# Second attention: the reciprocals of a pair of heads, spread over partitions by TensorE or by transfers through DRAM

## The chip, the cores and the metric

One core of one Trainium2 chip. The metric is the device time of one execution in microseconds; the time of before is the median of three runs, 1263.89 us (1263.47 to 1264.3).

## The reference, cut to what matters

Two layers of a decoder with 512 positions and 1024 features, in float32. The second layer's mixer is an attention of 16 heads over 128 latent columns, each query keeping its best keys by an indexer. What the change touches is the end of its softmax:

```
logits = einsum(q, k) * scale + bias         # per head: 512 queries x up to 512 keys
p = softmax(logits, axis=-1)                 # exp(l - max) / sum over keys
o_lat = einsum(p, lat)
o = einsum(o_lat, w_uv)                      # 64 columns per head
```

The kernel computes exp(l - max) without dividing, takes the weighted sum of the values, and multiplies the result by the reciprocal of the sum.

## The kernel before, in words

Scores are kept with 128 queries on partitions and the keys along a row; a head has four query blocks j = 0 to 3, of 128, 256, 384 and 512 keys (causal). The sums, and so their reciprocals, stand as a [128 x 4] tile: query within the block on partitions, block along the row. The output is wanted the other way round: two heads at a time ("a pair"), 64 output columns of each on 128 partitions and the 512 queries along the row. So each pair's 2 x 512 reciprocals must become a [128 x 512] tile `bs` in which the rows 0 to 63 all hold the first head's 512 reciprocals and 64 to 127 the second's.

The loop `for h in range(HEADS)` (L1537) does the end of head h together with the scores and the softmax of head n = h + 1, in one order that is written out by hand; each engine works its queue in that order. Per head:

- `logits` (L1427) writes scores z on TensorE (PE) for a block, in one of two PSUM banks of tag "z"; `softmax` (L1430) turns them on VectorE (DVE) into L and the row minima nm (L1436, L1438); `expo` (L1441) takes the exponential on ScalarE (ACT, L1444) and its sum. Blocks 0 and 1 come first, blocks 2 and 3 after the filler `fill(mid)`; the exponential of block 3 comes last.
- `transposed` (L1448) turns head h's exponentials on PE in three groups (L1455) and copies them out (L1460 on ACT, L1462 on DVE).
- In odd heads `pair_values` (L1466) multiplies the latent rows by two heads' columns into `pv` (L1470), copied out as `vals` by ACT (L1474). In even heads `weighted` (L1476) forms the pair's output `av` for the two heads before.
- `sums` (L1532) takes the reciprocals; after an odd head `pair_sums` (L1490) copies each reciprocal 64 times into `rvb` (L1492, DVE). In the next even head `pair_scale` (L1497) transposes rvb four times into `bc` (L1501, PE) and copies it out as `bs` (L1503, ACT). `pair_hi` (L1505) multiplies av by bs (L1507) and rounds (L1510), `pair_lo` (L1513) keeps the rest (L1514).
- `fill` (L1387) puts steps of a projection between (`pt_q`, later `pt_o`; three matmuls a step), `serve` and `serve_late` (L1401, L1410) the vector work that goes with them, with `q_sum` (L1124), the split of the next weight chunk (`whi`, L208) and the fetch of the one after it (L177). `load_bias` (L1183) loads a head's bias tile `th` from DRAM. All transfers here are issued by SyncE (SP), in order.

PSUM has eight banks: three of tag "mm", two "z", two "tr", and a single one "x" (L132), which ssq (of `q_sum`), pv and bc take in turn. A tile can be allocated there only when the one before it has been read out.

Of the kernel before, what the change touches and what calls it, by code (L numbers as in the profile page):

```python
# [9 lines left out]
F32 = mybir.dt.float32  # L10
# [3 lines left out]
AF = mybir.ActivationFunctionType  # L14
# [6 lines left out]
S = 512  # L21
P = 128
KT = D // P
QT = S // P
# [4 lines left out]
HEADS = 16  # L29
# [90 lines left out]
def kernel_body(ctx, tc, xT, wst, cst, smalls, crow, ccol, relb, onehot, outT):  # L120
    nc = tc.nc
    act, dve, pe, pool = nc.scalar, nc.vector, nc.tensor, nc.gpsimd
# [11 lines left out]
    def ptile(shape, name, tag):  # L134
        return banks.tile(shape, F32, name=name, tag=tag, bufs=nbanks[tag])
# [3 lines left out]
    ident = cons[:, C_ID:C_ID + P]  # L139
# [11 lines left out]
    x = [xpool.tile([P, S], F32, name=f"x{f}") for f in range(KT)]  # L151
    halves = [slice(0, H2), slice(H2, S)]

    dp = ctx.enter_context(tc.tile_pool(name="dram", bufs=1, space=DRAM))
    rb = dp.tile([HEADS, 640], F32, name="rb")

    rel = cpool.tile([BUCKETS, HEADS], F32, name="rel")
    bias = {}
# [927 lines left out]
    def dsa_layer(l, first, man):  # L1086
        with ExitStack() as st:
# [36 lines left out]
            def q_sum(h):  # L1124
                q2 = Q.pop((h, 2))
                ssq = ptile([P, QT], "ssq", "x")
                for j in range(QT):
                    pe.matmul(ssq[:, j:j + 1], lhsT=q2[:, j * P:(j + 1) * P], rhs=ones1, start=True, stop=True)
                c = slice(h * QT, (h + 1) * QT)
                act.activation(msq[:, c], ssq, AF.Identity, scale=1.0 / P, bias=eps_c)  # L1130
# [52 lines left out]
            def load_bias(h):  # L1183
                th = ths[h] = raws.tile([P, D], F32, name="th", tag="raw")[:, :S]
                ov = rb[h:h + 1, 0:1]
                nc.sync.dma_start(th, bass.AP(tensor=ov.tensor, offset=ov.offset, ap=[[1, P], [1, S]]))
# [164 lines left out]
            with ExitStack() as sa:  # L1351
                ap = sa.enter_context(tc.tile_pool(name="att_d", bufs=2))
# [4 lines left out]
                heads = {}  # L1357
# [29 lines left out]
                def fill(n):  # L1387
                    for _ in range(n):
                        next(filler, None)

                def take():

                    if lows:
                        lows.pop(0)()
                    else:
                        split_lo()
                    for done in finished:
                        done()
                    finished.clear()

                def serve():  # L1401

                    for h in ripe:
                        q_sum(h)
                        scales.append(h)
                    ripe[:] = squares
                    squares.clear()
                    take()

                def serve_late():  # L1410

                    for h in scales:
                        q_norm(h, h + 1)
                    scales.clear()
                    take()
                    if chunks["n"]:
                        split_hi()
                        chunks["n"] -= 1

                def begin(h):  # L1420
                    L = ap.tile([P, LW], F32, name="L")
                    if h % 2 == 0:
                        rv = ap.tile([P, QT, 2], F32, name="rv", bufs=4)
                        heads["rv"] = rv
                    heads[h] = (L, ap.tile([P, QT], F32, name="nm"), ap.tile([P, QT], F32, name="sum"), heads["rv"], {})

                def logits(h, j):  # L1427
                    heads[h][4][j] = score_block(h, j)
# [12 lines left out]
                def expo(h, j):  # L1441
                    L, nm, sum_ = heads[h][:3]
                    ls = slice(LOFF[j], LOFF[j] + (j + 1) * P)
                    act.activation(L[:, ls], L[:, ls], AF.Exp, bias=nm[:, j:j + 1], scale=-1.0, accum_out=sum_[:, j:j + 1])  # L1444
# [3 lines left out]
                def transposed(h, pi, by_act):  # L1448
                    L = heads[h][0]
                    tr = ptile([P, S], "tr", "tr")  # L1450
                    w = TRW[pi]
                    for i, c0 in TRP[pi]:
                        for j in range(i, QT):
                            c = c0 + (j - i) * P
                            pe.transpose(tr[:, c:c + P], L[:, LOFF[j] + i * P:LOFF[j] + (i + 1) * P], ident)  # L1455
                    if pi == 0:
                        trs[h] = ap.tile([P, LW], F32, name="pT", bufs=2)
                    t = trs[h][:, TRO[pi]:TRO[pi] + w]
                    if by_act:
                        act.activation(t, tr[:, :w], AF.Copy)  # L1460
                    else:
                        dve.tensor_copy(t, tr[:, :w])  # L1462
# [26 lines left out]

                def pair_sums(rv):  # L1490
                    rvb = ap.tile([P, QT, 2, 64], F32, name="rvb", tag="bs")
                    dve.tensor_copy(rvb, rv[:, :, :, None].to_broadcast([P, QT, 2, 64]))  # L1492
                    return rvb

                pair = {}

                def pair_scale(rvb):  # L1497

                    bc = ptile([P, S], "bc", "x")
                    for j in range(QT):  # L1500
                        pe.transpose(bc[:, j * P:(j + 1) * P], rvb[:, j].rearrange("p a b -> p (a b)"), ident)  # L1501
                    bs = pair["bs"] = ap.tile([P, S], F32, name="bs")
                    act.activation(bs, bc, AF.Copy)  # L1503

                def pair_hi():  # L1505
                    bs = pair["bs"]
                    dve.tensor_mul(bs, pair["av"], bs)  # L1507
                    oh = pp.tile([P, S], F32R, name="ohi", tag="qh", bufs=QRING)
                    ol = pp.tile([P, S], F32R, name="olo", tag="ql", bufs=QRING)
                    act.activation(oh, bs, AF.Copy)  # L1510
                    O.append((oh, ol))

                def pair_lo():  # L1513
                    dve.tensor_sub(O[-1][1], pair["bs"], O[-1][0].bitcast(F32))  # L1514

                load_bias(2)
                begin(0)
                heads[0][4].update(early)
                for j in range(2):
# [7 lines left out]
                    expo(0, j)  # L1527
                fill(4)
                serve_late()
                rvb = None  # L1530

                def sums(h):  # L1532

                    dve.reciprocal(heads[h][3][:, :, h % 2], heads[h][2])
                    return pair_sums(heads[h][3]) if h % 2 else None

                for h in range(HEADS):  # L1537
                    n = h + 1
                    more = n < HEADS
                    values = h % 2 == 0 and h > 0  # L1540
                    mid, after = LATE_STEPS[h]
                    if more:
                        begin(n)
                        for j in range(2):
                            logits(n, j)
                        softmax(n, 0)
                        expo(n, 0)
                    if values:
                        weighted(h - 2)
                    transposed(h, 0, True)  # L1550
                    if more:
                        softmax(n, 1)
                        expo(n, 1)
                    if h % 2 and h > 1:
                        pair_lo()
                    serve()
                    if not more:
                        rvb = sums(h)
                        pair_values(h - 1)
                    fill(mid)  # L1560
                    if more:
                        for j in range(2, QT):
                            logits(n, j)
                            softmax(n, j)
                            if j < QT - 1:
                                expo(n, j)
                    transposed(h, 1, False)
                    if values:
                        pair_scale(rvb)
                    if more:  # L1570
                        rvb = sums(h)
                        if h % 2:
                            pair_values(h - 1)
                        expo(n, QT - 1)
                    transposed(h, 2, True)
                    if not more:
                        pair_scale(rvb)
                    elif n + 2 < HEADS:
                        load_bias(n + 2)
                    fill(after)  # L1580
                    serve_late()
                    if values:
                        pair_hi()
                weighted(HEADS - 2)
                pair_hi()
# [124 lines left out]
```

## Time and profile before

| | us |
|---|---|
| median of three runs | 1263.89 |
| the profiled execution | 1263.59 |
| its span, first to last instruction | 1261.8 |
| PE busy | 1253.6 |
| DVE busy | 926.2 |
| ACT busy | 584.4 |
| second attention's loop over heads, about | 759 to 874 of the span |

Every row of a trace gives a start and a duration in microseconds from the span's start. A matmul's duration reaches past the start of the next one, since matmuls are pipelined; distances between starts tell what one costs. An arrow in brackets names what ended an engine's idle time.

### The profile page before, as it was taken

The numbers are of one execution on the slowest core, as the hardware profiler recorded it, in microseconds if no ns is written. First come the engines' busy times: TensorE is split into PE (matmuls) and PEld (weight loads), VectorE is DVE, ScalarE is ACT, GpSimd is POOL, SyncE is SP. The second block draws the span as 40 slices with busy tenths as digits, with TensorE's granted clock in tenths as the row PEclk, the third lists the DMA queues.
The fourth block names the chain that finished last, engine by engine and source line by source line (L and its number), as shares of the span: only waits on it lengthen the run. The fifth ranks groups of instructions, "written<-read, shape, count | busy, mean of one in ns | idle before, by whom it ended". The sixth has DMA issues, their size and how long they took to land.

```text
span 1261.8 us, 17355 instructions
## 1 busy us (share of the span) xinstructions
PE 1253.6 (99%) x6566; PEld 1037.4 (82%) x6566; DVE 926.2 (73%) x1575; ACT 584.4 (46%) x1029; POOL 57.2 (5%) x171
## 2 busy tenths in 40 slices
PE   8999999999999999999999999999999999999999
PEld 5888787798888888888887788887988888888887
DVE  5889998878777877886768878887875456456653
ACT  6477666554323433433445446656544234334330
POOL 0000000000000000000002350110000000000000
PEclk9999999999999999999999999999999999999999
DMA  9644444514575575654412222133232422433221
GB/s 375 219 136 132 136 134 125 173 37 125 198 254 181 181 245 188 200 182 153 134 34 68 84 76 69 59 95 103 72 92 75 133 86 70 129 87 97 76 92 67
DMA packets 49316, 163.13 MB, mean 129 GB/s; under 512 B 5664, under 2 KB 6176, under 8 KB 49232
## 3 DMA queue, kind: packets, MB, share of 16 engines
q1 hardware_dynamic: 48800, 161.23, 40.0%
q8 instruction: 52, 0.85, 0.3%
q10 hardware_dynamic: 432, 0.79, 0.2%
q14 instruction: 32, 0.26, 0.1%
HBM read 159.86 MB, written 2.14 MB: 128 GB/s over the span
## 4 chain that ended last, share of the span: by engine, by line
PE 95%; DVE 3%; DMA 1%; issue 0%; ACT 0%; ACTq 0%; SPq 0%; DVEq 0%
PE pt_u L248 12%; PE pt_u L250 12%; PE pt_u L249 11%; PE pt_d L250 5%; PE pt_d L248 5%; PE pt_d L249 5%; PE pt_l L248 2%; PE pt_q L248 2%; PE pt_l L250 2%; PE pt_l L249 2%; PE pt_first L248 2%; PE pt_q L250 2%; PE pt_first L250 2%; PE pt_q L249 2%; PE pt_first L249 2%; PE pt_qk L248 1%
## 5 line engine op out<-in xcount | busy, mean ns | idle before, releaser
L208 ACT ACTIVATE whi<-raw 128x1024 fp32r<-128x1024 f32 (+1 forms) x206 | 205.0, 1003 | 118.7 <-PE pt_d L250 89.2
L248 PE MATMUL pt_u<-hhi,whi 128*128 128x512 f32 x640 | 249.2, 389 | 0.0
L249 PE MATMUL pt_u<-hhi,wlo 128*128 128x512 f32 x640 | 249.0, 389 | 0.0
L250 PE MATMUL pt_u<-hlo,whi 128*128 128x512 f32 x640 | 249.0, 389 | 0.0
L216 DVE TENSOR_TENSOR wlo<-raw,whi 128x1024 fp32r<-128x1024 f32 (+1 forms) x194 | 223.3, 1153 | 9.4 <-ACT whi L208 8.4
L1021 ACT ACTIVATE y<-pt_u,sm 128x512 f32<-128x512 f32 x80 | 62.2, 777 | 188.2 <-PE pt_u L250 188.2
L248 PEld LDWEIGHTS pt_u<-hhi,whi 128*128 128x128 f32 x640 | 120.1, 188 | 25.8 <-issue 1.1
L250 PEld LDWEIGHTS pt_u<-hlo,whi 128*128 128x128 f32 x640 | 120.1, 188 | 25.0
L249 PEld LDWEIGHTS pt_u<-hhi,wlo 128*128 128x128 f32 x640 | 120.1, 188 | 24.9
L1022 DVE SCALAR_TENSOR_TENSOR y<-pt_u,sm,y 128x511 f32<-128x511 f32 x80 | 59.9, 748 | 97.1 <-ACT y L1021 96.9
L248 PE MATMUL pt_d<-acthi,whi 128*128 128x512 f32 x288 | 112.0, 389 | 0.0
L249 PE MATMUL pt_d<-acthi,wlo 128*128 128x512 f32 x288 | 112.0, 389 | 0.0
L250 PE MATMUL pt_d<-actlo,whi 128*128 128x512 f32 x288 | 112.0, 389 | 0.0
L257 DVE SCALAR_TENSOR_TENSOR raw<-raw,cond 128x1024 f32<-128x1024 f32 x88 | 106.5, 1216 | 4.2 <-DMA raw<-wst 4.2
L375 DVE SCALAR_TENSOR_TENSOR x<-pt_d,mod,x 128x512 f32<-128x512 f32 x48 | 36.0, 749 | 72.8 <-PE pt_d L250 72.8
L232 ACT ACTIVATE acthi<-y 128x512 fp32r<-128x512 f32 x44 | 27.8, 632 | 105.4 <-DVE y L1040 105.4
L248 PE MATMUL pt_first<-hhi,whi 128*128 128x256 f32 (+1 forms) x200 | 64.0, 320 | 0.0
L249 PE MATMUL pt_first<-hhi,wlo 128*128 128x256 f32 (+1 forms) x200 | 62.8, 314 | 0.8 <-DVE wlo L216 0.8
L249 PEld LDWEIGHTS pt_d<-acthi,wlo 128*128 128x128 f32 x288 | 54.1, 188 | 11.3
L250 PEld LDWEIGHTS pt_d<-actlo,whi 128*128 128x128 f32 x288 | 54.1, 188 | 11.2
L248 PEld LDWEIGHTS pt_d<-acthi,whi 128*128 128x128 f32 x288 | 54.1, 188 | 11.2
L250 PE MATMUL pt_first<-hlo,whi 128*128 128x256 f32 (+1 forms) x200 | 63.0, 315 | 0.0
(258 smaller groups left out, 2505.3 us busy)
## 6 DMA issues: line engine op xcount, KB each, us to landing
raw<-wst SPq DMA_DIRECT2D x250, 512.0 KB, 3.7
raw<-wst SPq DMA_DIRECT2D x48, 384.0 KB, 3.0
th<-rb SPq DMA_DIRECT2D x16, 256.0 KB, 3.1
ada<-wst SPq DMA_DIRECT2D x4, 512.0 KB, 6.6
outT<-x SPq DMA_DIRECT2D x7, 256.0 KB, 2.0
x<-xT SPq DMA_DIRECT2D x5, 256.0 KB, 4.9
x<-xT ACTq DMA_DIRECT2D x3, 256.0 KB, 4.0
cond<-crow SPq DMA_DIRECT2D x1, 512.0 KB, 10.4
```

What stands on the lines that cost most here:

```text
L208: act.activation(hi[:, :n], raw[:, :n], AF.Copy)
L216: engine.tensor_sub(lo[:, :n], raw[:, :n], hi[:, :n].bitcast(F32))
L232: act.activation(hi, src, AF.Copy)
L248: pe.matmul(out, lhsT=whi, rhs=ahi, start=start, stop=False)
L249: pe.matmul(out, lhsT=wlo, rhs=ahi, start=False, stop=False)
L250: pe.matmul(out, lhsT=whi, rhs=alo, start=False, stop=stop)
L257: dve.scalar_tensor_tensor(raw, raw, 1.0, cond, op0=OP.mult, op1=OP.mult, accum_out=dst)
L375: dve.scalar_tensor_tensor(x[f][:, c], pt, mod[l][:, g * KT + f:g * KT + f + 1], x[f][:, c], op0=OP.mult, op1=OP.add)
L1021: act.activation(y, pt, AF.Identity, scale=cw[2], bias=sm[:, b + S_CB + c:b + S_CB + c + 1])
L1022: dve.scalar_tensor_tensor(y[:, 1:], pt[:, :S - 1], cw[1], y[:, 1:], op0=OP.mult, op1=OP.add)
```

## The change

For all pairs but the last, the reciprocals no longer go through rvb and bc. The tile rv is laid out with the head ahead of the block; `sums` only takes the reciprocal, and is called before `fill(mid)`. In odd heads `pair_rows` is called between the scores of block 3 and the second group of transposes: one transpose of the [128 x 8] tile rv into `tp`, a PSUM tile of tag "x"; a copy by ACT into `r8`, [8 x 128]; and a write of that to a DRAM tile `rd`. After `load_bias` of the same head `pair_spread` reads rd back twice, each head's row of 512 into 64 partitions of `bs`. `pair_hi` of the next even head takes that tile. The last pair, for which no further head comes, keeps `pair_sums` and `pair_scale`.

```
+    rd = dp.tile([HEADS, S], F32, name="rd")
...
-                        rv = ap.tile([P, QT, 2], F32, name="rv", bufs=4)
+                        rv = ap.tile([P, 2, QT], F32, name="rv", bufs=4)
...
+                def pair_rows(h, rv):
+
+                    tp = ptile([P, S], "tp", "x")
+                    pe.transpose(tp[:2 * QT, :P], rv.rearrange("p e j -> p (e j)"), ident)
+                    r8 = ap.tile([P, P], F32, name="r8", bufs=1)[:2 * QT]
+                    act.activation(r8, tp[:2 * QT, :P], AF.Copy)
+                    row = rd[h:h + 1, 0:1]
+                    nc.sync.dma_start(bass.AP(tensor=row.tensor, offset=row.offset, ap=[[P, 2 * QT], [1, P]]), r8)
+
+                def pair_spread(h):
+                    bs = pair["next"] = ap.tile([P, S], F32, name="bs")
+                    for e in range(2):
+                        row = rd[h + e:h + e + 1, 0:1]
+                        nc.sync.dma_start(bs[64 * e:64 * e + 64, :], bass.AP(tensor=row.tensor, offset=row.offset, ap=[[0, 64], [1, S]]))
...
                 def sums(h):
-                    dve.reciprocal(heads[h][3][:, :, h % 2], heads[h][2])
-                    return pair_sums(heads[h][3]) if h % 2 else None
+                    dve.reciprocal(heads[h][3][:, h % 2], heads[h][2])
...
                     serve()
+                    sums(h)
                     if not more:
-                        rvb = sums(h)
+                        rvb = pair_sums(heads[h][3])
                         pair_values(h - 1)
                     fill(mid)
                     if more:
...
+                        if h % 2:
+                            pair_rows(h - 1, heads[h][3])
                     transposed(h, 1, False)
-                    if values:
-                        pair_scale(rvb)
                     if more:
-                        rvb = sums(h)
                         if h % 2:
                             pair_values(h - 1)
                         expo(n, QT - 1)
...
                         load_bias(n + 2)
+                    if more and h % 2:
+                        pair_spread(h - 1)
                     fill(after)
                     serve_late()
                     if values:
+                        if more:
+                            pair["bs"] = pair.pop("next")
                         pair_hi()
```

## Rows read from the trace of the kernel before

**Rows 1.** The page: busy time of PE with its share of the span and its instructions, and the chain that ended last, by engine.

```profile
PE 1253.6 (99%) x6566; PEld 1037.4 (82%) x6566; DVE 926.2 (73%) x1575; ACT 584.4 (46%) x1029; POOL 57.2 (5%) x171
...
PE 95%; DVE 3%; DMA 1%; issue 0%; ACT 0%; ACTq 0%; SPq 0%; DVEq 0%
```

**Rows 2.** Windows of one pair of heads each: the window, its length, busy time (and instructions) of PE, PE's weight loads, DVE, ACT and POOL, then the granted clock, the DMA share and GB/s. The shortest and the longest of six.

```profile
766.00:780.30 14.30, 14.30 (x95) 11.61 (x93) 10.91 (x31) 9.29 (x27) 2.74 (x13) 1.00 0.13 32
...
824.80:842.40 17.60, 17.60 (x111) 14.51 (x110) 15.41 (x41) 10.14 (x30) 4.01 (x13) 1.00 0.34 99
```

**Rows 3.** What ended idle time from 755 to 890 us: engine, line, releaser, then us in total, times and the longest.

```profile
ACT L L1444 <- DVE nm L1438: 31.5, 29, 2.5
DVE L L1436 <- PE z L1178: 13.9, 9, 2.5
...
PE bc L1501 <- DVE rvb L1492: 0.2, 1, 0.2
```

**Rows 4.** The timeline in head 3: pv on PE, the first softmax instruction of block 2 of head 4 on DVE, its exponential and then `vals` on ACT.

```profile
776.88 1.06 PE L1470 MATMUL pv<-uvc,latf 128*128 128x128 f32 x8
...
777.84 0.61 DVE L1436 SCALAR_TENSOR_TENSOR L<-z,cols,th 128x384 f32<-128x384 f32 x1
...
779.09 0.62 ACT L1444 ACTIVATE L<-L,nm 128x384 f32<-128x384 f32 x1 [1.13 <-DVE nm L1438]
...
779.70 0.64 ACT L1474 ACTIVATE vals<-pv 128x256 f32<-128x256 f32 x2
```

**Rows 5.** The groups of instructions that the change removes from all pairs but the last: count, busy us and mean ns of one, idle time before them.

```profile
L1501 PE MATMUL bc<-cons,rvb 128*128 128x128 f32 x32 | 4.8, 273 | 0.2 <-DVE rvb L1492 0.2
L1503 ACT ACTIVATE bs<-bc 128x512 f32<-128x512 f32 x8 | 4.6, 581 | 0.4 <-PE bc L1501 0.4
...
L1492 DVE COPY rvb<-rv 128x512 f32<-128x512 f32 x8 | 3.4, 427 | 0.3
```

**Rows 6.** The chain of waits, the piece of the transposes bc in head 2: start, us on the chain.

```profile
771.52 0.44 PE bc L1501 x4
```

**Rows 7.** The timeline of PE: pv in heads 1, 5, 7, 9, 11 and 13.

```profile
763.62 1.06 PE L1470 MATMUL pv<-uvc,latf 128*128 128x128 f32 x8
...
791.91 1.06 PE L1470 MATMUL pv<-uvc,latf 128*128 128x128 f32 x8
...
806.80 1.16 PE L1470 MATMUL pv<-uvc,latf 128*128 128x128 f32 x8
...
820.87 1.06 PE L1470 MATMUL pv<-uvc,latf 128*128 128x128 f32 x8
...
838.46 1.06 PE L1470 MATMUL pv<-uvc,latf 128*128 128x128 f32 x8
...
855.21 1.06 PE L1470 MATMUL pv<-uvc,latf 128*128 128x128 f32 x8
```

**Rows 8.** The timeline of ACT: `vals` in heads 1, 5, 7, 9 and 11, and for head 13 the instruction ahead of it.

```profile
764.71 0.66 ACT L1474 ACTIVATE vals<-pv 128x256 f32<-128x256 f32 x2
...
793.46 0.64 ACT L1474 ACTIVATE vals<-pv 128x256 f32<-128x256 f32 x2
...
808.29 0.64 ACT L1474 ACTIVATE vals<-pv 128x256 f32<-128x256 f32 x2
...
823.68 0.64 ACT L1474 ACTIVATE vals<-pv 128x256 f32<-128x256 f32 x2
...
840.43 0.64 ACT L1474 ACTIVATE vals<-pv 128x256 f32<-128x256 f32 x2
...
856.05 0.19 ACT L1444 ACTIVATION_READ_ACCUMULATOR L<-L,nm 128x1 f32 x1
```

**Rows 9.** Small copies out of PSUM by ACT: that of ssq in head 7 in the timeline, and the group of copies of 128x256.

```profile
806.50 0.25 ACT L1130 ACTIVATE cols<-ssq,ecols 128x4 f32<-128x4 f32 x1
...
L1460 ACT ACTIVATE pT<-tr 128x256 f32<-128x256 f32 x16 | 5.8, 364 | 0.3 <-PE tr L1455 0.3
```

**Rows 10.** The timeline of DVE: its wait for the scores of block 2 in an even head (2) and in an odd one (13).

```profile
770.42 0.62 DVE L1436 SCALAR_TENSOR_TENSOR L<-z,cols,th 128x384 f32<-128x384 f32 x1 [2.20 <-PE z L1178]
...
854.27 0.62 DVE L1436 SCALAR_TENSOR_TENSOR L<-z,cols,th 128x384 f32<-128x384 f32 x1 [0.32 <-PE z L1178]
```

**Rows 11.** The last matmul of the kernel in the timeline, and two windows behind it: window, length, PE's busy time, granted clock, DMA share, GB/s.

```profile
1258.43 0.28 PE L250 MATMUL pt_l<-actlo,whi 128*128 128x256 f32 x1
...
1260.50:1261.00 0.50, 0.00 (x0) 0.76 0.04 10
1261.00:1261.80 0.80, 0.00 (x0) 0.50 0.00 0
```

**Rows 12.** DMA issues of the whole kernel: count, KB each, median us from issue to landing.

```profile
th<-rb SPq DMA_DIRECT2D x16, 256.0 KB, 3.1
...
rb<-rsb SPq DMA_DIRECT2D x1, 40.0 KB, 1.7
head<-ccol SPq DMA_DIRECT2D x1, 4.0 KB, 2.6
```

**Rows 13.** The timeline: the use of bs in head 4 by DVE; the issue of a weight load by SP, and the first instruction on ACT that uses what it brought.

```profile
788.91 0.69 DVE L1507 TENSOR_TENSOR bs<-av,bs 128x512 f32<-128x512 f32 x1
...
832.55 0.33 SPq L177 DMA_DIRECT2D raw<-wst  x1
...
842.19 1.04 ACT L208 ACTIVATE whi<-raw 128x1024 fp32r<-128x1024 f32 x1
```

More of the change, by code (lines that the diff above doesn't have):

```diff
@@ L1491, in pair_sums @@
                     rvb = ap.tile([P, QT, 2, 64], F32, name="rvb", tag="bs")
-                    dve.tensor_copy(rvb, rv[:, :, :, None].to_broadcast([P, QT, 2, 64]))
+                    dve.tensor_copy(rvb, rv.rearrange("p e j -> p j e")[:, :, :, None].to_broadcast([P, QT, 2, 64]))
                     return rvb
@@ L1529, in dsa_layer @@
                 serve_late()
-                rvb = None
                 def sums(h):
-                    dve.reciprocal(heads[h][3][:, :, h % 2], heads[h][2])
-                    return pair_sums(heads[h][3]) if h % 2 else None
+                    dve.reciprocal(heads[h][3][:, h % 2], heads[h][2])
                 for h in range(HEADS):
```

## The prediction

> **What bounds it.** I read the page's busy shares first: TensorE is busy 99% of the span, and the chain that ended last is 95% PE [rows 1]. A stage of 105 us is what the change touches, so I read that stage next, in windows of one pair of heads: 14.3 to 17.6 us a pair, and PE busy in all of it [rows 2]. Busy is not proof, so the third view is what ended the idle time of each engine from 755 to 890 us. PE waits 0.2 us in all that time. VectorE (DVE) waits 13.9 us for z from PE, ScalarE (ACT) 31.5 us for DVE's row minima [rows 3]. The reader is to see that PE never waits because it runs ahead: the softmax work reaches DVE and ACT a few us after PE has written z, and nothing that PE needs soon hangs on them.
>
> How far ahead is the number that decides here. In head 3 (an odd head, `n` = 4) PE reaches `pair_values` at 776.88. DVE starts the softmax of block 2 of the next head only at 777.84, ACT its exponential at 779.09 after 1.13 us of waiting for that, and ACT's next instruction, `vals`, starts at 779.70 [rows 4]. That is the order in which the code writes them, and ACT does not take `vals` first although pv has been written since 777.94 (776.88 and 1.06 us).
>
> **The change, part by part.** *Removed* in heads 2, 4 to 14: the broadcast copy rvb (DVE, 427 ns), four transposes bc (PE) and the copy bs (ACT, 581 ns) [rows 5]. The last pair keeps the old way. On PE the four transposes take 0.44 us of the chain, 0.11 us each [rows 6]. On DVE and ACT the removed work ends before waits of theirs (for z, for the minima), so it counts as nothing: after rvb DVE soon waits for z in the even head, after bs ACT still waits for its minima.
>
> *Added* per odd head 1 to 13: one transpose tp (0.11 us, as one of bc's), one copy r8 on ACT of 8 partitions by 128 columns, one write of 4 KB and two reads of 128 KB on SP. The reciprocal goes up on DVE, in front of the softmax of blocks 2 and 3, in both heads of a pair: what it adds to the odd stretch it takes from the even one, zero net.
>
> *The new wait.* tp is allocated in the PSUM tag "x", which has one bank, and so is pv right after it. tp goes into PE's queue behind z of block 3, and pv four transposes later. So pv's first matmul now waits until r8 has emptied the bank, and r8 stands in ACT's queue behind the exponential of block 2, which waits for DVE. In the code of before pv only found a bank that had been emptied long since. What is queued behind it on PE: everything, that is the last transposes, the fill, the next z, on which DVE then waits in turn.
>
> The size: r8 starts where `vals` started, and I subtract PE's arrival at pv. Seven odd heads, from [rows 4, 7, 8]: 764.71-763.62 = 1.09; 779.70-776.88 = 2.82; 793.46-791.91 = 1.55; 808.29-806.80 = 1.49; 823.68-820.87 = 2.81; 840.43-838.46 = 1.97; in head 13 `vals` itself waited for pv, so I take the end of the accumulator read there, 856.05 and 0.19: 856.24-855.21 = 1.03. Sum 12.76 us.
>
> To that comes r8 and the release. r8 has no row. The copy of 128x4 out of the x bank takes 0.25 us, that of 128x256 0.364 [rows 9]; by columns 128 lies halfway, 0.30. The release has one: in head 7 the bank was last used by ssq, ACT emptied it from 806.50 to 806.75 [rows 9], pv came at 806.80 and its eight matmuls took 1.16 us instead of 1.06 [rows 7]. That is the same wait in small: PE loses about 0.15 us after ACT's end. So 0.45 a pair, 3.15 in seven. Bounds: 0.25 and 0.05 make 0.30, 0.364 and 0.3 make 0.66, so 2.1 to 4.6.
>
> Does the delay go to the end? In every even head DVE waits for z (2.20 us in head 2 [rows 10]): PE's lateness becomes DVE's lateness there, then DVE works on without slack to the next softmax of block 2, and PE has its lead again when it meets the next pv. So each pair pays anew. For the same reason most of bc's 0.44 us buys nothing: PE comes earlier to a wait that DVE and ACT end. It helps where DVE waits for z in an odd head too, head 13 with 0.32 us [rows 10], and about 0.1 at the end, where the chain goes over DVE and one reciprocal leaves it. That is 0.4 us back: 12.76 + 3.15 - 0.4 = 15.5 us later.
>
> *The clock.* In heads 3 to 13 PE also arrives 0.33 us earlier (0.44 less 0.11), so its idle stretches would be about 1.5, 3.6, 2.3, 2.3, 3.6, 2.8 and 1.8 us, nearly 18 in all. The trace has one long one, at the end: the last matmul ends at 1258.71, and the mean of 0.76 from 1260.5 to 1261.0, with 0.50 after it, puts the fall of the granted clock to one half at 1260.76, after 2.05 us [rows 11]. If the same befalls the two stalls of 3.6 us and the clock stays low for about as long as it took to be noticed (3 us of work, half of it lost), that is 1.5 us each, 3.0 together. The bounds are no such dip, 0, and one at each of the seven, 1.7 us each, 11.9. I take two: both stalls are well beyond 2.05 us, the others near it. [...]
>
> *The transfers* I cost at nothing. r8 ends at about 780.0 in head 3; a 4 KB load at the start landed in 2.6 us, the 40 KB write to rb in 1.7, th's 256 KB in 3.1 [rows 12]. So bs is there 5 to 6 us later, and DVE multiplies by it only at 788.91, itself moved by 3 us. On SP the reads wait for the write to land, and the weight loads stand behind them, up to 3.3 us late (2.6 and two issues of 0.33). The shortest lead that I find is from an issue at 832.55 to its use at 842.19, 9.6 us [rows 13]. If that cover were gone, whi would be late next. `vals` and the exponential of block 3 now follow pv on ACT, some 1.5 us later, but their readers come in the next head, and PE is as late.
>
> **The sum.** The profiled execution took 1263.59 us, 0.30 under the median. 1263.59 + 15.5 + 3.0 = 1282.1; at the median's level 1282.4.
>
> **Rivals.** *A, no stall.* The program that fills the queues might put r8 ahead of the exponential of block 2. It decides by whether the copy is out of the bank within the 0.43 us of transposes between tp and pv. Then PE keeps 0.33 us in seven pairs, 2.3 us: 1261.6. For it: nothing in r8 needs DVE's late work. Against it: `vals` could have gone first in the same way, and did not in head 3; ACT's idle time stands before the exponential.
>
> *B, the clock falls at every stall.* For it: 2.05 us was enough once. Against it: four of the stalls are at or under 2.3 us. 1263.9 + 15.5 + 11.9 = 1291.3.
>
> *C, the transfers are late.* If write and reads took over 12 us, DVE would wait at bs in the even heads, behind which stands its whole softmax: 2 us in seven pairs, 14 more, 1296. Against it: the landing times of 1.7 to 3.1 us.
>
> *D, half a stall.* If DVE, relieved of rvb and bs, came to block 2 about 1 us sooner in every pair, 15.5 would shrink to about 8.5: 1272.4. Against it: its wait for z in the even heads sets it back to PE each time.
>
> **Chances.** Forecast 0.63, A 0.14, B 0.10, C 0.04, D 0.09. Over 0.2% (2.5 us) is about what a measurement of this kernel can tell. A's 2.3 us lies within that, mostly: same 0.11, faster 0.04, slower 0.85. The forecast's own bounds go from 1278 (no dip, cheap copies) to 1287; D and B belong in the range as far as they reach, and C and A stay out: 1271 to 1291.
>
> **What would show it.** Right: in the rows of waits PE's first matmul of pv waits for ACT's r8, about 1.5 to 3.6 us in each of seven odd heads, nearly 18 in all; PE's busy share of the stage falls to some 85%; DVE's wait for z in the stage rises by about the same, and bs is never waited for. The granted clock shows 0.5 at two places between 775 and 850. Wrong: r8 before the exponential of block 2 in ACT's order (A); pv starting less than 0.2 us after the transposes; DVE waiting for a DMA before its product with av (C); or a stage that is longer by the 15 us without any wait at pv.

## The result, and the profile after

The changed kernel takes 1281.14 us (median of five runs, 1279.05 to 1284.9) against 1263.89: a ratio of 1.0138 (95% interval 1.0127 to 1.0149). It is slower by 17.3 us; 18.5 had been forecast. Its runs differ more than those of before, and in step with the granted clock: 1279.05 us at a mean clock of 1.000, 1279.81 at 0.999, 1281.14 at 0.997, 1282.58 at 0.996, 1284.90 at 0.995. The profiled execution is the last of these.

The page of the changed kernel, the lines that answer to [rows 1]:

```profile
PE 1260.5 (98%) x6545; PEld 1038.5 (81%) x6545; DVE 924.3 (72%) x1568; ACT 582.4 (45%) x1029; POOL 58.0 (5%) x171
...
PE 91%; DVE 5%; ACT 1%; DMA 1%; issue 1%; SPq 0%; DVEq 0%; ACTq 0%
```

PE has 21 instructions fewer, DVE and ACT are busy for less, and the chain has moved by 4 points from PE to DVE, ACT and "issue". What ended idle time from 755 to 900 us (engine, line, releaser, us in all, times, longest), as in [rows 3]; the line numbers of the second attention are one to some twenty higher than before:

```profile
DVE L L1437 <- PE z L1179: 32.0, 15, 4.5
...
PE pv L1471 <- ACT r L1511: 8.2, 7, 1.3
...
PE tp L1509 <- DVE rv L1548: 4.8, 4, 1.8
...
PE tp L1509 <- ACT cols L1131: 0.3, 1, 0.3
```

PE, which waited 0.2 us in this stage before, waits 13.3 us, at two places; DVE's wait for z rises by 18.1 us, as PE is late for it. No row names a DMA. Head 3 in the timeline, first PE, then DVE, then ACT; this answers to [rows 4]:

```profile
777.71 0.39 PE L1179 MATMUL z<-kpl,qh 128*128 128x512 f32 x1
779.89 0.27 PE L1509 MATMUL tp<-cons,rv 128*8 128x128 f32 x1 [1.80 <-DVE rv L1548]
780.00 0.60 PE L1456 MATMUL tr<-cons,L 128*128 128x128 f32 x4
781.89 1.39 PE L1471 MATMUL pv<-uvc,latf 128*128 128x128 f32 x6 [1.29 <-ACT r L1511]
```

```profile
778.46 0.69 DVE L1530 TENSOR_TENSOR olo<-bs,ohi 128x512 fp32r<-128x512 f32 x1 [0.93 <-ACT ohi L1526]
779.07 0.69 DVE L1122 TENSOR_TENSOR ql<-pt_q,qh 128x512 fp32r<-128x512 f32 x1
779.67 0.17 DVE L1548 RECIPROCAL rv<-sum 128x4 f32<-128x4 f32 x1
779.75 0.59 DVE L1437 SCALAR_TENSOR_TENSOR L<-z,cols,th 128x384 f32<-128x384 f32 x1
```

```profile
780.98 0.61 ACT L1445 ACTIVATE L<-L,nm 128x384 f32<-128x384 f32 x1 [1.20 <-DVE nm L1439]
781.50 0.19 ACT L1445 ACTIVATION_READ_ACCUMULATOR L<-L,nm 128x1 f32 x1
781.59 0.25 ACT L1511 ACTIVATE r<-tp 8x128 f32<-8x128 f32 x1
```

PE finishes z of block 3 and stands still at tp, since DVE takes the reciprocal only behind the rounding remainder of the pair before (olo), for which it waited 0.93 us itself, and the split of another head (ql); then it does tr, and stands still again until ACT has emptied tp's bank (`r` is r8), which comes behind the exponential that waits for DVE. From r8's start (781.59) to pv's first matmul it is 0.30 us.

The granted clock, in windows of 3.41 us whose edges are laid at the instants where it changes (window, length, PE's busy time and instructions, granted clock, DMA share, GB/s):

```profile
778.80:782.21 3.41, 1.03 (x7) 1.00 0.00 0
782.21:785.62 3.41, 3.41 (x14) 0.50 0.50 144
785.62:789.04 3.42, 3.42 (x25) 1.00 0.32 95
...
830.00:833.41 3.41, 1.27 (x8) 1.00 0.00 0
833.41:836.82 3.41, 2.46 (x11) 0.50 0.20 57
836.82:840.24 3.42, 3.42 (x10) 0.50 0.85 169
...
853.89:857.30 3.41, 1.16 (x8) 1.00 0.00 0
857.30:860.72 3.42, 3.42 (x14) 0.50 0.53 137
```

After each of the stalls in heads 3, 9 and 11 PE works at half clock for 3.4 or 6.8 us, four windows in all.

### The profile page after: what moved, and what is told of

The parts are those of the page before. It is cut to its first block, busy times and chain, and to the rows that moved or that the text cites. A ratio compares the mean times of both kernels' runs of the same rounds, so it can differ in the third digit from the quotient of the medians.

```text
span 1283.1 us, 17354 instructions
## 1 busy us (share of the span) xinstructions
PE 1260.5 (98%) x6545; PEld 1038.5 (81%) x6545; DVE 924.3 (72%) x1568; ACT 582.4 (45%) x1029; POOL 58.0 (5%) x171
## 4 chain that ended last, share of the span: by engine, by line
PE 91%; DVE 5%; ACT 1%; DMA 1%; issue 1%; SPq 0%; DVEq 0%; ACTq 0%
PE pt_u L249 11%; PE pt_u L251 11%; PE pt_u L250 11%; PE pt_d L251 5%; PE pt_d L249 5%; PE pt_d L250 5%; PE pt_l L249 2%; PE pt_l L250 2%; PE pt_l L251 2%; PE pt_first L249 2%; PE pt_first L251 2%; PE pt_q L249 2%; PE pt_first L250 2%; PE pt_q L250 2%; PE pt_q L251 2%; PE pt_qk L249 1%
```

## The experiments

Ratios are to runs of the kernel before that were taken beside each experiment; their medians are 1264.27 us for e1 to e4, 1264.03 for e5 to e8 and 1264.75 for e9 and e10. "The stage" is 755 to 900 us of the span.

**The bank alone (e1).**

```
-                    tp = ptile([P, S], "tp", "x")
+                    tp = ptile([P, S], "tp", "mm")
```

> The changed kernel with one word changed: tp is allocated in the PSUM tag with three banks, so pv no longer shares a bank with it. Theory 1 (PE waits for the single bank, which ACT empties late): the 8.2 us of waits at pv go; what stays is PE's wait at tp for the reciprocal, by the rows of before about 1.6 us in heads 3 and 9, 0.7 in 11, 0.2 to 0.3 in 5 and 7, some 4 us: about 1268 us. Theory 2 (the transfers and their queue cost the time): no change, about 1281. Theory 3 (the reciprocal put ahead of the softmax on DVE costs the time): about 1281.

Measured: 1268.46 us, ratio to before 1.0032 (1.002 to 1.0044). The waits of PE in the stage:

```profile
PE tp L1509 <- DVE rv L1548: 4.9, 5, 1.8
```

The wait at pv is gone and the one at tp stays. A single word brings the loss from 17.3 us down to 4.2, and the transfers are all still there: theory 2 falls.

**The transpose and its copy without transfers (e2).** The kernel before with the early reciprocals, and in odd heads, at the place of the change:

```
+                    tp = ptile([P, S], "tp", "x")
+                    pe.transpose(tp[:2 * QT, :P], rv.rearrange("p e j -> p (e j)"), ident)
+                    r8 = ap.tile([P, P], F32, name="r8", bufs=1)[:2 * QT]
+                    act.activation(r8, tp[:2 * QT, :P], AF.Copy)
```

> The kernel before with only the early reciprocals, tp (in the single bank) and its copy r8 added; no transfer at all, and the old way over rvb, bc and bs kept, so r8 is read by nobody. Theory 1: all of the loss is here, 1279 to 1282 us, and bc's transposes, still there, cost next to nothing more. Theory 2: 1264. Theory 3: about 1281 as well, which the next run but one tells apart.

Measured: 1281.42 us, ratio 1.0139 (1.0124 to 1.0154), with rvb, bc and bs still at work. All of the loss comes with these four lines and the early reciprocal (which e4 tries by itself), and bc's transposes beside them make no difference that can be measured: PE would only have waited longer.

**The reciprocals alone (e4).** The kernel before, with `sums` called ahead of the filler and rv in the new layout; `pair_sums` stays where it was.

> The kernel before with only the new layout of rv and the reciprocals moved ahead of the filler; rvb, bc and bs as before. Theory 1: 1263.9 us, within 0.5. Theory 2: 1263.9. Theory 3: later by most of the 17 us.

Measured: 1264.04 us, ratio 1.0 (0.9991 to 1.0009). Theory 3 falls: the place of the reciprocal on DVE costs nothing that can be measured.

**The early reciprocal with the single bank (e10).**

```
+                    sums(h)
                     if h % 2 and h > 1:
                         pair_lo()
                     serve()
-                    sums(h)
```

> The changed kernel with the reciprocal taken ahead of the rounding and the split work of its head, tp still in the single bank. PE no longer waits at tp, and comes to pv that much sooner. Theory 1 (r8's place behind the late exponential sets when pv starts, whatever PE does ahead of it): the wait moves from tp to pv, some 13 us there, and the time stays at 1279 to 1282. If the two waits were separate costs: 1281 less 4.8, about 1276.

Measured: 1282.25 us, ratio 1.0139 (1.0122 to 1.0155). What ended PE's idle time in the stage:

```profile
PE pv L1471 <- ACT r L1511: 13.5, 7, 3.2
PE tp L1509 <- ACT cols L1131: 0.3, 1, 0.3
```

The wait for the reciprocal is gone, and pv's wait has grown from 8.2 to 13.5 us. The two waits of the changed kernel are one lateness, whose end r8 sets.

**r8 ahead of the exponential (e7).**

```
                             if j < QT - 1:
+                                if h % 2:
+                                    pair_rows(h - 1, heads[h][3])
                                 expo(n, j)
-                        if h % 2:
-                            pair_rows(h - 1, heads[h][3])
```

> The changed kernel with tp, r8 and the write called between the softmax of block 2 and its exponential: r8 stands ahead of the exponential in ACT's queue, the bank is still the single one. Theory 1: pv's wait goes, for r8 no longer waits for DVE's minima; PE waits at tp for the reciprocal instead, and reaches tp 0.7 us earlier, ahead of block 3's scores. By the rows of before the lateness is 0.2, 2.4, 0.9, 0.9, 2.2, 1.3 and 0 us in heads 1 to 13, 7.9 in all: about 1271. Rival (it is the single bank alone, wherever r8 stands): 1281.

Measured: 1274.03 us, ratio 1.0077 (1.0063 to 1.0091): 10.0 us over before, where 7 to 8 were expected. The waits at tp in the trace:

```profile
PE tp L1509 <- DVE rv L1548: 8.0, 5, 2.5
...
PE tp L1509 <- ACT cols L1131: 1.3, 1, 1.3
PE tp L1509 <- DVE L L1437: 0.7, 1, 0.7
```

The wait at pv is gone with the bank unchanged, so it is not the bank alone but r8's place behind the late exponential. That the 8.0 us agree with the 7.9 worked out is luck: they stand at five heads, for which 6.8 had been worked out (heads 3, 5, 9, 11 and 13, each 0.1 to 0.4 us longer), and in head 7, where 0.9 had been, PE waits 1.3 us for the same bank while ssq holds it. The 0.7 us for L, in head 1, had been put at 0.2.

**More work for PE (e6).**

```
+                    for _ in range(8):
-                    pe.transpose(tp[:2 * QT, :P], rv.rearrange("p e j -> p (e j)"), ident)
+                        pe.transpose(tp[:2 * QT, :P], rv.rearrange("p e j -> p (e j)"), ident)
```

> The changed kernel with the transpose tp done eight times over (the same values into the same place), so PE works 0.77 us longer in each of seven odd heads, between its two waits. Theory 1 with slack at pv: the waits at pv (0.83 to 1.29 us) shrink by 0.77 and the time does not grow; where the clock stays high, 1279 as the changed kernel's fastest run; and since less of a stretch is idle the low-clock stretches become fewer, so the median lies at or under 1281. Rival (PE's work in the stage counts in full): 5.4 us more, about 1286.

Measured: 1278.75 us (1278.4 to 1279.01), ratio 1.0115 (1.0099 to 1.013), and a clock of 1.000 in all four runs. PE's wait at pv is down to

```profile
PE pv L1471 <- ACT r L1512: 2.7, 6, 0.5
```

49 transposes more, 5.4 us of PE's work, and the kernel is 2.4 us under the median of the changed one and no slower than its fastest run (1279.05): PE's time at this place was idle, and with it filled the clock stayed up.

**No transpose at all (e3).**

```
-                    tp = ptile([P, S], "tp", "x")
-                    pe.transpose(tp[:2 * QT, :P], rv.rearrange("p e j -> p (e j)"), ident)
-                    r8 = ap.tile([P, P], F32, name="r8", bufs=1)[:2 * QT]
-                    act.activation(r8, tp[:2 * QT, :P], AF.Copy)
...
+                        nc.sync.dma_start(bass.AP(tensor=row.tensor, offset=row.offset, ap=[[1, P], [P, 2 * QT]]),
+                                          rv.rearrange("p e j -> p (e j)"))
```

> The changed kernel without tp and r8: the write to DRAM takes rv as it stands, 1024 numbers of 4 bytes each to its own place; the two reads as in the changed kernel. Theory 1: no new wait on PE, and bc's 0.44 us saved in seven pairs, 3.1 us: about 1261 us, if the write lands within some 6 us (else DVE waits for bs). Theory 2: 1281 or more, since the transfers are the same and the write is in smaller pieces. Theory 3: about 1278.

Measured: 1286.11 us, ratio 1.0175 (1.0161 to 1.0189). My expectation was wrong by its own condition. The issues (count, KB, median us to landing), and what ended idle time in the stage:

```profile
bs<-rd SPq DMA_DIRECT2D x14, 128.0 KB, 3.2
rd<-rv SPq DMA_DIRECT2D x7, 4.0 KB, 10.7
```

```profile
DVE bs L1521 <- DMA bs<-rd: 17.4, 6, 4.3
...
PE z L1177 <- DVE L L1437: 14.5, 5, 3.9
```

The transpose is gone, and with it PE's waits at tp and pv. But the write in pieces of 4 bytes lands after 10.7 us. DVE waits for bs at the end of the even head, its softmax stands behind that wait, and PE then waits for the z banks that DVE has not emptied. This is rival C of the prediction, brought about by another write.

**The rows later (e5).** tp in the three-bank tag; `pair_rows` and `pair_spread` both behind the odd head's `fill(after)`.

```
-                        if h % 2:
-                            pair_rows(h - 1, heads[h][3])
...
-                    if more and h % 2:
-                        pair_spread(h - 1)
                     fill(after)
+                    if more and h % 2:
+                        pair_rows(h - 1, heads[h][3])
+                        pair_spread(h - 1)
```

> The changed kernel with tp in the three-bank tag, and the rows' transpose, copy, write and reads called after the odd head's last filler instead of ahead of the second group of transposes. PE comes to tp about 3 us later, when the reciprocal has long been taken, and r8 stands behind the last copy of ACT. Theory 1 (both of PE's waits gone, nothing new): bc's 0.44 less tp's 0.11 in seven pairs, 2.3 us under before: 1261.6 to 1262. Transfers late (a rival for this order): the write and the reads need some 4.5 us (issue to issue 1.2, landing 3.0 in the changed kernel), against about 7 us to the use in head 4, so no wait; if they were later, DVE would wait at bs as in the run with pieces of 4 bytes, and the time would be over 1264.

Measured: 1265.51 us, ratio 1.0009 (1.0 to 1.0018): not faster. The timeline at the start of head 10, PE and ACT:

```profile
823.96 0.27 PE L1509 MATMUL tp<-cons,rv 128*8 128x128 f32 x1
...
825.92 2.37 PE L1488 MATMUL av<-pT,vals 128*64 128x512 f32 x16 [1.01 <-ACT r L1511]
```

```profile
825.36 0.36 ACT L1461 ACTIVATE pT<-tr 128x256 f32<-128x256 f32 x1
825.62 0.25 ACT L1511 ACTIVATE r<-tp 8x128 f32<-8x128 f32 x1
```

It is the same fault in another place: av waits for r8 to empty a bank of the three, and r8 stands behind `vals`, the exponential of block 3 and the last copy in ACT's queue. PE waits there in three heads, 1.7 us in all. With the 1.0 us that e8 shows the saving to be, that would make 0.7 us over before; 1.5 were measured, and where the other 0.8 lie was not traced.

**The other bank and the early reciprocal (e8).** The edits of e1 and e10 together.

> The changed kernel with tp in the three-bank tag and the reciprocal taken ahead of the rounding and the split work of its head on DVE. Theory 1: neither wait is left, at tp or at pv, so only the saving stays: 1261.6 us. If the reciprocal's place was not what PE waited for at tp: 1268 as with the bank alone.

Measured: 1263.04 us, ratio 0.999 (0.9981 to 0.9999), the only complete version that is not slower than before; the gain of 0.1% is half of what a single measurement can tell, and stands on eleven runs. PE waits at neither place. Of the 2.3 us expected 1.0 came. The timeline of PE in head 5:

```profile
790.68 0.34 PE L1179 MATMUL z<-kpl,qh 128*128 128x384 f32 x1
790.96 0.51 PE L1177 MATMUL z<-kph,qh 128*128 128x512 f32 x1
791.30 0.40 PE L1178 MATMUL z<-kph,ql 128*128 128x512 f32 x1
791.53 0.39 PE L1179 MATMUL z<-kpl,qh 128*128 128x512 f32 x1
```

The starts of block 3's scores are 0.28 and 0.34 us apart from the one before, where 0.17 and 0.23 is what they take without a wait (790.78 and 791.01 in the same head of the kernel before). PE comes to the z bank before DVE has emptied it. The weight loads of z on PE (PEld) show the wait in five heads, where the kernel before has none:

```profile
PEld z L1177 <- DVE L L1437: 1.2, 5, 0.3
```

**Nothing instead (e9).** The changed kernel without tp, r8 and the transfers; `pair_hi` of the seven pairs multiplies by `latf` in place of bs.

> The changed kernel without tp, r8 and all three transfers: for seven pairs nothing stands in the place of rvb, bc and bs, and av is multiplied by another tile of the same shape, so the division is left out. It measures the most that taking bc away can bring. If PE's own work is what bounds the stage, as my sum had it: 0.44 us in seven pairs, 3.1 less than before, 1260.9. If VectorE bounds it as well, through the two z banks that it empties (in the run with the other bank and the early reciprocal PE's z of block 3 starts up to 0.3 us late): about 1262 to 1262.5, no more than 0.5 to 1 us under that run's 1263.0.

Measured: 1262.61 us, ratio 0.9986 (0.9977 to 0.9994). Even with nothing in its place, taking bc away brings about 1.8 us (0.14% of 1264), not the 3.1 of PE's own work. The trace has the same wait as e8's, in five heads:

```profile
PEld z L1177 <- DVE L L1437: 1.3, 5, 0.4
```

DVE, through the z banks, is thus the second bound. These 1.3 us are waits of the weight loads; of waits for L, PE's own rows name 0.2 us, once. So the rows do not say how much of the missing 1.3 us they make.

## Why the prediction was right

- *PE waits at pv for r8 in ACT's queue, because of the single bank.* Shown: e2 has the whole loss without a transfer, e1 is rid of most of it with another bank, e7 of 7 us with another place of r8. Rival A did not come: in head 3 r8 starts at 781.59, behind the exponential at 780.98.
- *The size, 15.5 us without the clock.* The changed kernel's run at clock 1.000 took 1279.05 us, 15.2 over before. The subtraction of PE's arrivals from the starts of `vals` held, and head by head: in e6, where the clock stays up, pv starts at 764.84, 781.38, 798.21, 814.99, 832.26, 852.23 and 869.90 us, and its lateness against [rows 4, 7] grows by 3.28, 1.80, 1.89, 3.20, 2.38 and 0.92 from head 3 to head 13. The prediction's differences with 0.45 added, and with 0.32 off in head 13, are 3.27, 2.00, 1.94, 3.26, 2.42 and 1.16. So each pair pays anew, as forecast. r8 and the release were put at 0.45 us; measured are 0.30 from r8's start to pv's and 0.10 in pv's longer group (1.16 us against 1.06 in heads without a low clock), 0.40: the copy took 0.25, not 0.30.
- *Where PE waits.* Wrong in part: I let tp pass unhindered and put the whole stall at pv. 5.1 of the 13.3 us lie at tp, 4.8 of them for a reciprocal that I had placed on DVE's path but not asked who waits for. It did not change the sum, since r8 comes later than both (e10). But it hid that two things have to be mended: the bank alone leaves 4 us (e1).
- *The waits add up to nearly 18 us.* The profile counts 13.3. A matmul's modelled end reaches past the next start (tp is shown with 0.27 us and costs 0.11), which takes some 0.16 us off each of the 12 waits, about 1.9 us; the rest of the difference was not traced. For the same reason PE is busy for 100.73 of the 113 us from 762 to 875, 89%, where some 85 had been forecast. DVE's wait for z, up by 18.1, is nearer, though it takes in the low clock too.
- *The clock, two low stretches, 3.0 us.* The median shows 2.1 (1281.14 - 1279.05), the profiled execution 5.9 with four windows, 1.5 each as forecast; e6 takes them away. The 3 us of work behind the 1.5, and the 1.7 us a stall in the upper bound, were my estimates, and no run shows them; the stretches at half clock measured here lasted 3.41, 6.83 and 3.42 us. The number of two is luck. By the mean clocks the five runs had about 0, 1, 2, 3 and 4 windows at half clock (an estimate: one of 3.41 us takes 0.0013 off the mean over 1281 us), and in the profiled one head 11, with a shorter stall, was hit as well as heads 3 and 9. The row at the end of the kernel [rows 11] had it right that about 2 us of idleness can be enough: the windows of 3.41 us ahead of the falls at 782.21, 833.41 and 857.30 had 1.03, 1.27 and 1.16 us of PE's work in them, so 2.1 to 2.4 us without.
- *bc's saving counts as nothing here, 0.4 us.* Right while PE waits (e2 against the changed kernel). But rival A's price, 2.3 us, was too high: with no stall 1.0 comes (e8), and 1.8 with nothing instead (e9).
- *The transfers cost nothing.* Right: DVE never waits for bs from DRAM. From the write's issue to the first read's it is 1.2 us (765.31 to 766.53 in head 1), and the reads land after 3.0. Rival C would have needed 12 us; e3, with 10.7 for the write alone, shows what it looks like. B did not come: heads 1, 5, 7 and 13 show no low clock in the profiled execution. D is excluded by the 15.2 us.

## What to carry to other kernels

Before a tile goes into a PSUM tag with one bank, look for who takes that bank next, and where in its engine's queue the copy stands that empties it: here a 0.25 us copy behind an instruction that waited for a third engine held TensorE for up to 1.3 us a head, 8.2 us in seven (3.2 and 13.5 in e10). An engine that is never idle because it runs ahead of the others has that lead to lose; the price of a new wait can be read from the profile of before, as the difference between its arrival and the start of the instruction behind which the releaser will stand. Moving the tile to another tag or place asks the same question again (e5).

## What the runs showed of the hardware

In these traces the falls of the TensorE clock went with how little PE had worked in the 3.41 us ahead of them. In the changed kernel 3.41 us is the shortest stretch at half clock, and the six changes of the clock in this stage (782.21, 785.62, 833.41, 840.24, 857.30 and 860.72) lie 1, 14, 2, 5 and 1 times as far apart. Over the windows of that length that ran at full clock in this stage (the traces of the kernel before, the changed one and all experiments but e4; edges laid by each trace's own changes of the clock; PE's work as the profile counts it), the next window was at half clock after each of the ten with up to 1.50 us of PE's work, and at full after every one with 1.58 or more. The nearest of either kind, from e3 and e7:

```profile
795.17:798.58 3.41, 1.50 (x10) 1.00 0.43 142
798.58:802.00 3.42, 3.29 (x11) 0.50 0.11 1
```

```profile
774.88:778.29 3.41, 1.58 (x10) 1.00 0.00 0
778.29:781.70 3.41, 2.76 (x20) 1.00 0.18 37
```

The fall at the end of the kernel before, from which the prediction took its 2.05 us, fits: the window ahead of it, 1257.34 to 1260.76, had 1.37 us of work. Once the clock was down, three windows with 2.30 to 2.52 us of work (e3, the changed kernel, e10) were each followed by another at half clock, and the ten with 2.83 (e2) or more by full clock; so a stall could cost two windows.

In the profiled execution of the changed kernel the stalls of heads 3, 9 and 11 thus cost, beside their own length, one or two windows at half clock, 1.5 us each (1284.90 - 1279.05 = 5.85 us over four), and those of the other four heads nothing more. That it depends on where a stall lies against the windows is my reading of it; each kernel left one trace. The number of windows accounts for the scatter: the changed kernel's runs spread over 5.9 us, in step with the clock, and those of e6, with PE's idle time in part filled, over 0.6. A write of 4 KB took 10.7 us to land in pieces of 4 bytes; with pieces of 512 bytes its reader was issued 1.2 us after it.
